# Four gate tiles of a convolution's input as one unit of seven half-size products, behind the query projection

## The chip, the core and the metric

The kernel runs on one core of a Trainium2 chip, as one launch. The metric is the device time of one execution in microseconds (us). A core has five engines that run side by side and wait for each other by semaphores: TensorE (PE in the profile; its weight loads are listed as PEld), VectorE (DVE), ScalarE (ACT), GpSimd (POOL) and SyncE (SP, which here only issues DMAs).

## What is computed

A decoder layer over 512 tokens of width 1024: half a SwiGLU feed-forward step, a token mixer, half a second feed-forward step, and a gated embedding. All inputs and results are float32. The change lies in the mixer:

```python
h = rmsnorm(x, mix_norm[i])
z = h @ w_in[i]
zq, zk, zv, zc, zg = [z[..., offs[j]:offs[j + 1]] for j in range(len(SPLIT_SIZES))]
...
a = sliding_window_attention(q, k, v, sinks[i]) @ attn_proj[i]

ca, cb = jnp.split(zc, 2, axis=-1)
u = ca * jax.nn.sigmoid(cb)
u = causal_depthwise_conv(u, dw_w[i], dw_b[i])
c = jax.nn.silu(layernorm(u, conv_ln_g[i], conv_ln_b[i])) @ conv_proj[i]

ga, gb = jnp.split(zg, 2, axis=-1)
merged = jax.nn.sigmoid(ga) * a + jax.nn.sigmoid(gb) * c
x = x + merged @ w_out[i]
```

There are 16 query heads and 2 key/value heads of 64, a window of 128 tokens, and a depthwise convolution of 31 taps over 1024 channels. `ca` and `cb` are 1024 channels wide each, so 8 tiles of 128 channels.

## The kernel before

**How a product is made.** Activations are kept with channels on the 128 partitions and 512 tokens along the free axis, in 8 tiles (`KD`). Every float32 operand is split into a high part and a rest (`split_into`), and a product is three matmuls: high by high, high by rest, rest by high (`mm3`). A plain projection (`proj`) of one tile of 128 output channels is 8 k-tiles by 3 matmuls of 512 columns into one PSUM bank. Its weight piece is 128 by 1024. For the pieces of `wzc` and `wzg` (`residue`), ACT makes the high part and the negated high part, and a DMA issued by POOL adds the raw piece to the latter; DVE has no part in it.

**A unit.** `unit` computes two by two blocks of weights against two by two blocks of activations with seven products in place of eight, after Strassen's method. Blocks are halves of the contraction and halves of the outputs on the weight side, and halves of the contraction and halves of the tokens (256 each, `lo_` and `hi_`) on the other. The seven sums of the activations are handed to it as `forms`; the seven sums of the weights it makes itself: four blocks are loaded (`raw`, three, and `k`, one), two DMAs add a block onto another, DVE adds into two PSUM tiles (`zs`), and each of the seven is split by ACT (high) and DVE (rest). Products come in the order 1 and 2, 6 and 5, 7 and 3, then 4, each for `nm` = 2 column groups; each is 4 k-tiles by 3 matmuls of 256 columns here. After each pair the caller gets the PSUM banks b1 and b2 and joins them. With nm = 2 a unit holds four such banks beside the two `zs`. Both feed-forward steps, the output projection, half of the query projection (`query_unit`, which also makes the seven sums of the mixer's input) and part of the last gate are made by units.

**The convolution.** Step `a` of channel tile c (`conv_in`) projects ca into a PSUM bank, which stays held (`pas[c]`). Step `b` (`conv_gate`) projects cb, multiplies by the norm's factor `rb2` (DVE), takes the sigmoid (ACT), multiplies by `rb2` again (POOL), multiplies by the held ca into u (DVE), and starts `conv`. `conv` adds the 31 taps: for c = 0, 2, 4 (`POOLCH`) ACT scales (tiles `ct`) and POOL adds; for the other five DVE does each tap in one operation on a PSUM bank (`cz`). Step `L` (`conv_norm`) sums all channels, spreads the mean (`ln_mb` on PE), subtracts it, sums squares (`ln_v_cs`), spreads the reciprocal root (`ln_v_sp`) and makes `cv`, the operand of the last projection of the mixer (`cp`).

**The order.** `ORDER` is a list of steps by hand: K keys and values, Q queries, A scores, E softmax, V values, a and b as above, g and h the two output gates, p the attention's projection, L the layer norm. The steps are only recorded. A planner (`plan`, `simulate`) then lays out all instructions: it has a cost for each kind, a due time for each operation (`deadlines`), a count of buffers (`SLOTS`: 70 general ones of class `a`, 4 `raw`, 4 `hi`, 4 `lo`, 2 `k`, 8 PSUM banks), and for PE it looks up to ten groups of matmuls ahead (`WINDOW`) for one that is ready. It keeps the best of several passes and the instructions are issued in the order that it found. Each engine runs its own in that order, so a late instruction holds up all behind it on its engine. Operations on `nc.flex` go to DVE or POOL as the planner finds best. Where DVE and POOL would both read their shared way to the buffers, it adds a wait of POOL on DVE by hand (`turns`).

Since all instructions are issued at one place, the profile gives L1778 for nearly all of them; they are told apart by the names of their tiles: `ca`, `cb` for the two projections, `wq_a`, `wq_b` for the query unit's two sorts of bank, `q1b` for the other half of the queries, `sc`, `pT`, `o` for attention.

Of the kernel before, what the change touches and what calls it, by code (L numbers as in the profile page):

```python
# [12 lines left out]
AF = mybir.ActivationFunctionType  # L13
ALU = mybir.AluOpType
AX = mybir.AxisListType

P = 128
# [3 lines left out]
KD = D // P  # L21
# [12 lines left out]
PIECE = 1024  # L34
# [3 lines left out]


ORDER = """  # L40
K0 a0 b0 a1 b1 Q0 A0 a3 a2 A1 b2 E0 E1 b3 A2 E2 a4 V0 A3 a5 E3 V1 b4 Q1 V2 b5
V3 A5 a7 A6 g5 h7 A4 E5 A7 E6 E4 V6 g3 a6 E7 g0 V5 b6 V4 g4 g6 V7 h1 g2 h4 b7
g1 p0 p2 g7 p3 L0 p4 h3 p7 h2 p5 p1 p6 h5 h0 h6
"""
POOLCH = (0, 2, 4)
WARM = 9

# [641 lines left out]
def record():  # L689
# [5 lines left out]
    def ftile(name):  # L695
        return nc.tile(name, [P, S], F32, "a")
# [531 lines left out]
    def proj(tag, key, i, h, nk=KD):  # L1228

        w = piece(key, i)  # L1230
        ps = ps_tile(tag)
        with nc.group(tag):
            for k in range(nk):
                mm3(ps, part(w, slice(k * P, (k + 1) * P)), h[k], k == 0, k == nk - 1)
        return ps
# [23 lines left out]
                        mm3(ps, part(w, slice(k * P, (k + 1) * P)), h[k], k == DONE[0], k == DONE[-1])  # L1259
        return {o: ps for o, (w, ps) in out.items()}  # L1260

    us, ys, pas = [None] * KD, [None] * KD, [None] * KD

    def conv_in(c):
        pas[c] = proj(f"ca{c}", "wzc", 2 * c, h2)

    def conv_gate(c):
        pb = proj(f"cb{c}", "wzc", 2 * c + 1, h2)
        sg = ftile(f"sg{c}")
        nc.vector.tensor_tensor(sg, pb, rb2, op=ALU.mult)  # L1270
        nc.scalar.activation(sg, sg, AF.Sigmoid)
        nc.gpsimd.tensor_tensor(sg, sg, rb2, op=ALU.mult)
        us[c] = ftile(f"u{c}")
        nc.vector.tensor_tensor(us[c], pas[c], sg, op=ALU.mult)
        conv(c)

    def conv(c):
        u = us[c]  # L1280
# [35 lines left out]
    def rope(tag, z3, n, tab, t):  # L1316

        w = nc.tile(f"{tag}_w", [P, n, 16], F32, "a")
        cos = tab[:, t, 0].unsqueeze(1).broadcast_to([P, n, 16])
        for d in (0, 8):  # L1320
            sin = tab[:, t, 1, d : d + 8].unsqueeze(1).broadcast_to([P, n, 8])
            nc.gpsimd.tensor_tensor(w[:, :, d : d + 8], z3[:, :, 8 - d : 16 - d], sin, op=ALU.mult)
        nc.gpsimd.tensor_tensor(z3[:, :, 0:16], z3[:, :, 0:16], cos, op=ALU.mult)
        nc.gpsimd.tensor_tensor(z3[:, :, 0:16], z3[:, :, 0:16], w, op=ALU.add)
# [49 lines left out]

    zq, rq = {}, {}

    def query_unit(g):

        forms = {f: [] for f in range(1, 8)}
        for q in range(2):  # L1380
            t5, t6, t7, t4 = (ftile(f"mix_t{n}_{q}") for n in (5, 6, 7, 4))
            for j in range(2):
# [35 lines left out]
    def queries(g):  # L1418

        if g == 0:  # L1420
            query_unit(g)
        else:
            pss = token_major(f"q{g}", "wq", 4 * g, 4, 2, S)
            for t in range(NT):
                z = zq[g, t] = ftile(f"zq{g}_{t}")
                nc.scalar.activation(z, pss[t], AF.Copy, scale=r2k[:, t : t + 1])
        z3s = [zq[g, t].rearrange("p (h d) -> p h d", d=HD) for t in range(NT)]
        rq[g] = heads_rsqrt(f"q{g}", z3s, 8, HD**-0.5, False)
        for t in range(NT):
            rope(f"q{g}_{t}", z3s[t], 8, qcs, t)  # L1430

    state = {}

# [174 lines left out]
    def embedding(i):  # L1608
# [24 lines left out]
        "e": embedding,  # L1633
        "K": lambda n: keys_values(),
        "Q": queries,
        "a": conv_in,
        "b": conv_gate,
        "g": attn_gate,
# [144 lines left out]
def _layout(inputs):  # L1783
# [35 lines left out]
    def pairs(w):  # L1819
        t = kxn(w)  # L1820
        n = t.shape[0] // 2
        return t.reshape(2, n, *t.shape[1:]).transpose(1, 0, 2, 3).reshape(t.shape)

    wap = f["attn_proj"][0].reshape(NH, HD, D)[order].reshape(NH * HD, D)

    half = HD // 8
# [27 lines left out]
        "wd2": wdown(f["ffn2_wdown"][0]),  # L1854
        "wq": wq,
        "wkv": wkv,
        "wzc": pairs(win[:, o[3] : o[4]]),
        "wzg": pairs(win[:, o[4] : o[5]]),
        "gq": rows(f["q_norm"][0]),
        "gk": rows(f["k_norm"][0]),  # L1860
# [35 lines left out]
```

## Time and profile before

| | |
|---|---|
| median of 3 runs | 1145.6 us (1145.52 to 1145.76) |
| the profiled execution | 1145.5 us, of which the profile's span is 1143.8 |
| granted clock of TensorE, mean | 0.999 |
| busy in the span: PE, DVE, ACT, POOL | 99%, 87%, 65%, 40% |
| read from HBM, written | 145.59 MB, 2.10 MB |

Matmuls overlap in time, so the duration of one in the profile (389 ns for 512 columns) is longer than the distance from one to the next. What a group of matmuls costs is read from the chain that ended last, which gives each piece the time until the next one. An engine's idle time costs something only where the chain goes through it.

### The profile page before, as it was taken

The page shows a single profiled execution, that of the slowest core. Times are in us where ns is not written, and L with a number is a line of the kernel's source. Part 1 is how long each engine was busy: PE and PEld are TensorE (multiplying, and loading weights), DVE is VectorE, ACT ScalarE, POOL GpSimd, SP SyncE. Part 2 cuts the span into 40 slices and gives each one's busy share as a digit, 9 for nine tenths or more (in the row PEclk, how much of TensorE's full clock was granted, in tenths as well). Part 3 has the DMA queues.
Part 4 walks back from the last instruction along what each step waited for, and adds up shares of the span by engine and source line. Part 5 has one row for each costly group of instructions (what it writes and reads, how often), then busy time and mean ns, then how long its engine had stood idle before and what let it go on. Part 6 is the DMA issues. An engine that isn't in the chain of part 4 may idle for free.

```text
span 1143.8 us, 20799 instructions
## 1 busy us (share of the span) xinstructions
PE 1135.7 (99%) x7804; PEld 1054.2 (92%) x7804; DVE 1000.4 (87%) x1701; ACT 743.0 (65%) x1332; POOL 457.8 (40%) x531
## 2 busy tenths in 40 slices
PE   9999999999999999999999999999999999999998
PEld 8899999999999988888888888988999999999997
DVE  7799978889887799997997779989998788899897
ACT  7656456665557889999975654655663566565682
POOL 1632113322112896976688124035231132131156
PEclk9999999999999999999999999999999999999999
DMA  7456666665658481664644554436666666656643
GB/s 242 126 162 148 165 160 163 151 144 151 157 132 208 119 206 38 173 158 97 162 129 131 146 148 108 114 108 169 145 164 151 150 167 148 168 119 178 152 117 99
DMA packets 54821, 167.92 MB, mean 147 GB/s; under 512 B 6592, under 2 KB 14400, under 8 KB 54720
## 3 DMA queue, kind: packets, MB, share of 16 engines
q1 hardware_dynamic: 39888, 114.12, 30.2%
q0 software_dynamic: 14688, 52.44, 26.6%
q8 instruction: 61, 1.00, 0.4%
q14 instruction: 40, 0.33, 0.1%
q10 hardware_dynamic: 144, 0.03, 0.0%
HBM read 145.59 MB, written 2.10 MB: 129 GB/s over the span
## 4 chain that ended last, share of the span: by engine, by line
PE 97%; DVE 3%; issue 0%; ACT 0%; ACTq 0%
PE wgu_b L1778 17%; PE wgu_a L1778 13%; PE wd_b L1778 10%; PE wd_a L1778 8%; PE f_g L1778 5%; PE f_u L1778 5%; PE gb L1778 4%; PE ga L1778 4%; PE ap L1778 4%; PE cp L1778 4%; PE ca L1778 3%; PE cb L1778 3%; PE wout_b L1778 2%; PE pg L1778 2%; PE q1b L1778 2%; PE wout_a L1778 2%
## 5 line engine op out<-in xcount | busy, mean ns | idle before, releaser
L1778 DVE TENSOR_TENSOR wlo_wgu<-raw_wgu,whi_wgu 128x1024 fp32r<-128x1024 f32 (+1 forms) x141 | 140.4, 1010 | 27.1 <-ACT whi_wgu L1778 26.8
L1778 ACT ACTIVATE whi_wgu<-raw_wgu 128x1024 fp32r<-128x1024 f32 (+1 forms) x141 | 115.4, 838 | 69.8 <-PE wgu_b L1778 34.7
L1778 POOL TENSOR_TENSOR y<-y,ct 128x511 f32<-128x511 f32 (+26 forms) x90 | 112.0, 1319 | 14.1 <-ACT ct L1778 5.3
L1778 PE MATMUL wgu_b<-f_t_h,wlo_wgu 128*128 128x256 f32 x408 | 115.5, 283 | 0.0
L1778 PE MATMUL wgu_b<-f_t_h,whi_wgu 128*128 128x256 f32 x408 | 115.5, 283 | 0.0
L1778 PE MATMUL wgu_b<-f_t_l,whi_wgu 128*128 128x256 f32 x408 | 115.5, 283 | 0.0
L1778 ACT ACTIVATE whi_wd<-raw_wd 128x896 fp32r<-128x896 f32 (+1 forms) x60 | 59.3, 989 | 73.3 <-PE wd_b L1778 41.5
L1778 DVE SCALAR_TENSOR_TENSOR cz<-u,dww,cz 128x504 f32<-128x504 f32 (+28 forms) x145 | 104.7, 733 | 2.0
L1778 POOL DMA_DIRECT2D raw_wgu<-in_wgu x34 | 29.7, 878 | 153.3 <-DMA raw_wgu<-in_wgu 78.6
L1778 PEld LDWEIGHTS wgu_b<-f_t_h,wlo_wgu 128*128 128x128 f32 x408 | 78.3, 192 | 0.0
L1778 PEld LDWEIGHTS wgu_b<-f_t_h,whi_wgu 128*128 128x128 f32 x408 | 78.3, 192 | 0.0
L1778 PEld LDWEIGHTS wgu_b<-f_t_l,whi_wgu 128*128 128x128 f32 x408 | 78.3, 192 | 0.0
L1778 DVE TENSOR_TENSOR wlo_wd<-raw_wd,whi_wd 128x896 fp32r<-128x896 f32 (+1 forms) x60 | 70.8, 1180 | 7.2 <-ACT whi_wd L1778 6.8
L1778 PE MATMUL wgu_a<-f_nh,wlo_wgu 128*128 128x256 f32 x272 | 77.0, 283 | 0.0
L1778 PE MATMUL wgu_a<-f_nh,whi_wgu 128*128 128x256 f32 x272 | 77.0, 283 | 0.0
L1778 PE MATMUL wgu_a<-f_nl,whi_wgu 128*128 128x256 f32 x272 | 77.0, 283 | 0.0
L1778 PE MATMUL wd_b<-f_f_h,wlo_wd 128*128 128x256 f32 x264 | 75.1, 285 | 1.2 <-DVE x L1778 1.2
L1778 PE MATMUL wd_a<-f_f_h,wlo_wd 128*128 128x256 f32 x264 | 74.7, 283 | 0.0
L1778 PE MATMUL wd_a<-f_f_h,whi_wd 128*128 128x256 f32 x264 | 74.7, 283 | 0.0
L1778 PE MATMUL wd_b<-f_f_l,whi_wd 128*128 128x256 f32 x264 | 74.7, 283 | 0.0
L1778 PE MATMUL wd_b<-f_f_h,whi_wd 128*128 128x256 f32 x264 | 74.7, 283 | 0.0
L1778 PE MATMUL wd_a<-f_f_l,whi_wd 128*128 128x256 f32 x264 | 74.7, 283 | 0.0
(625 smaller groups left out, 4278.6 us busy)
## 6 DMA issues: line engine op xcount, KB each, us to landing
raw_wgu<-in_wgu SPq DMA_DIRECT2D x76, 512.0 KB, 4.5
raw_wgu<-in_wgu POOLq DMA_DIRECT2D x34, 512.0 KB, 5.5
raw_wd<-in_wd SPq DMA_DIRECT2D x32, 448.0 KB, 4.0
raw_wd<-in_wd SPq DMA_DIRECT2D x16, 512.0 KB, 4.4
raw_wzc<-in_wzc SPq DMA_DIRECT2D x16, 512.0 KB, 3.9
wlo_wzc<-raw_wzc POOLq DMA_DIRECT2D x16, 512.0 KB, 4.9
raw_wzg<-in_wzg SPq DMA_DIRECT2D x16, 512.0 KB, 3.5
wlo_wzg<-raw_wzg POOLq DMA_DIRECT2D x16, 512.0 KB, 4.5
```

Source lines behind the costliest of these rows:

```text
L1778: made[op] = getattr(engines[op.eng], op.what)(*a, **k)
```

## The change

The gates (cb) of channel tiles 2, 3, 4 and 5 leave their four steps `b2` to `b5` and become one step `U0`, a unit that stands right behind the first half of the queries, `Q0`. It takes the same seven sums of the mixer's input (`forms2`, made by `query_unit`). The four weight pieces are laid out anew on the host, so that each holds half of the contraction for two tiles. The unit leaves sigmoid gates in SBUF (`su2` to `su5`); the four steps `a2` to `a5` then multiply and convolve as soon as their own projection is there. The other gates (0, 1, 6, 7) stay as they are.

```diff
 ORDER = """
-K0 a0 b0 a1 b1 Q0 A0 a3 a2 A1 b2 E0 E1 b3 A2 E2 a4 V0 A3 a5 E3 V1 b4 Q1 V2 b5
+K0 a0 b0 a1 b1 Q0 U0 A0 a3 a2 A1 E0 E1 A2 E2 a4 V0 A3 a5 E3 V1 Q1 V2
 V3 A5 a7 A6 g5 h7 A4 E5 A7 E6 E4 V6 g3 a6 E7 g0 V5 b6 V4 g4 g6 V7 h1 g2 h4 b7
 g1 p0 p2 g7 p3 L0 p4 h3 p7 h2 p5 p1 p6 h5 h0 h6
 """
+UNITED = (2, 3, 4, 5)
...
     def conv_in(c):
         pas[c] = proj(f"ca{c}", "wzc", 2 * c, h2)
+        if c in UNITED:
+            convolve(c)
 
     def conv_gate(c):
         pb = proj(f"cb{c}", "wzc", 2 * c + 1, h2)
-        sg = ftile(f"sg{c}")
+        sg = sgs[c] = ftile(f"sg{c}")
         nc.vector.tensor_tensor(sg, pb, rb2, op=ALU.mult)
         nc.scalar.activation(sg, sg, AF.Sigmoid)
         nc.gpsimd.tensor_tensor(sg, sg, rb2, op=ALU.mult)
+        convolve(c)
+
+    def convolve(c):
         us[c] = ftile(f"u{c}")
-        nc.vector.tensor_tensor(us[c], pas[c], sg, op=ALU.mult)
+        nc.vector.tensor_tensor(us[c], pas[c], sgs[c], op=ALU.mult)
         conv(c)
...
+    forms2 = {f: [] for f in range(1, 8)}
+
     def query_unit(g):
 
-        forms = {f: [] for f in range(1, 8)}
+        forms = forms2
...
+    def gate_unit():
+
+        def src(b):
+            return Dram("wzc")[2 * UNITED[2 * (b // 10 - 1) + b % 10 - 1] + 1]
+
+        def finish(sg):
+            nc.flex.tensor_tensor(sg, sg, rb2, op=ALU.mult)
+            nc.scalar.activation(sg, sg, AF.Sigmoid)
+            nc.gpsimd.tensor_tensor(sg, sg, rb2, op=ALU.mult)
+
+        for f, m, b1, b2 in unit("gu", src, PIECE, lambda k, m: (m * 4 + k) * P, forms2):
+            if f == 1:
+                t, u = (ftile(f"su{UNITED[n]}") for n in (m, m + 2))
+                sgs[UNITED[m]], sgs[UNITED[m + 2]] = t, u
+                nc.scalar.copy(t[:, lo_], b1)
+                nc.vector.tensor_tensor(t[:, lo_], b2, t[:, lo_], op=ALU.add)
+            t, u = sgs[UNITED[m]], sgs[UNITED[m + 2]]
+            if f == 6:
+                nc.scalar.copy(t[:, hi_], b2)
+                nc.scalar.activation(u[:, hi_], b1, AF.Copy, scale=-1.0)
+            elif f == 7:
+                nc.vector.tensor_tensor(t[:, hi_], b1, t[:, hi_], op=ALU.add)
+                nc.vector.scalar_tensor_tensor(u[:, hi_], b2, -1.0, u[:, hi_], op0=ALU.mult, op1=ALU.add)
+                finish(t)
+            elif f == 4:
+                nc.scalar.activation(u[:, lo_], b2, AF.Copy, scale=-1.0)
+                finish(u)
...
+        "U": lambda n: gate_unit(),
...
+    at = [2 * u + 1 for u in UNITED]
+    wzc = pairs(win[:, o[3] : o[4]])
+    wu = wzc[at].reshape(2, 2, P, 2, 4, P).transpose(0, 3, 2, 1, 4, 5)
+    wzc[at] = wu.reshape(4, P, PIECE)
```

More of the change, by code (lines that the diff above doesn't have):

```diff
@@ L1260, in proj2 @@
         return {o: ps for o, (w, ps) in out.items()}
-    us, ys, pas = [None] * KD, [None] * KD, [None] * KD
+    us, ys, pas, sgs = ([None] * KD for _ in range(4))
     def conv_in(c):
         pas[c] = proj(f"ca{c}", "wzc", 2 * c, h2)
+        if c in UNITED:
+            convolve(c)
     def conv_gate(c):
         pb = proj(f"cb{c}", "wzc", 2 * c + 1, h2)
-        sg = ftile(f"sg{c}")
+        sg = sgs[c] = ftile(f"sg{c}")
         nc.vector.tensor_tensor(sg, pb, rb2, op=ALU.mult)
@@ L1856, in _layout @@
         "wkv": wkv,
-        "wzc": pairs(win[:, o[3] : o[4]]),
+        "wzc": wzc,
         "wzg": pairs(win[:, o[4] : o[5]]),
```

## The prediction

> **What bounds the kernel now.** I read the page's first part and its chain of work first, then what TensorE (PE) waited for over the whole span, then windows over the mixer.
>
> ```profile
> PE 1135.7 (99%) x7804; PEld 1054.2 (92%) x7804; DVE 1000.4 (87%) x1701; ACT 743.0 (65%) x1332; POOL 457.8 (40%) x531
> PE 97%; DVE 3%; issue 0%; ACT 0%; ACTq 0%
> PE wd_b L1778 <- DVE x L1778: 1.2, 4, 0.5
> PE ca L1778 <- DVE s L1778: 0.9, 1, 0.9
> 345.88:704.62 358.74, 357.60 (x1893) 301.60 (x1892) 310.15 (x562) 285.62 (x564) 235.71 (x304) 1.00 0.55 140
> ```
>
> PE is busy 99% of the span and is 97% of the chain that ended last. The last line is the mixer, from the first key/value matmul to the last of the convolution's projection; its columns are length, then busy time of PE, PEld, DVE, ACT and POOL, granted clock, DMA share and GB/s. PE idles 358.74 - 357.60 = 1.14 us there, at a granted clock of 1.00. So time is won in this stage only by giving PE less to stream, or from those 1.14 us, of which 0.9 us is one projection waiting for a PSUM bank that VectorE (DVE) had to empty of scores. DVE is second with 310 of 359 us.
>
> **What the change takes from PE.** The chain of waits, in order of time, has both forms of work: a query unit of seven products (wq) that is already in the kernel, and gate projections (cb).
>
> ```profile
> 381.00 1.43 PE wq_b L1778 x12
> ...
> 396.82 1.44 PE wq_a L1778 x12
> 398.26 5.47 PE ca L1778 x24
> 403.73 2.87 PE wq_b L1778 x24
> 406.60 5.47 PE cb L1778 x24
> ...
> 443.88 5.46 PE cb L1778 x24
> ...
> 450.67 5.46 PE cb L1778 x24
> ```
>
> One gate tile is 8 x 3 = 24 matmuls of 512 columns and costs 5.46 us, 0.2275 each. Four of them (the fourth lies at a place where the chain runs over DVE; I give it the same) cost 2 x 5.46 + 5.47 + 5.46 = 21.85 us. The new unit has the query unit's count: 7 products x 2 column groups x 4 k-tiles x 3 = 168 matmuls of 256 columns. The query unit ran six products from 381.00 to 398.26, without a gap, and the seventh in 2.87: 17.26 + 2.87 = 20.13 us, 0.1198 each. **PE saves 21.85 - 20.13 = 1.72 us**, all of it on the path that ends last.
>
> Why an eighth less arithmetic gives no eighth (2.73 us): from 0.2275 = a + 512 b and 0.1198 = a + 256 b, a column costs b = 0.42 ns and a matmul a = 12 ns whatever its width. The change removes 96 x 512 - 168 x 256 = 6144 columns (2.6 us) and adds 72 matmuls (0.9 us).
>
> The Trainium skill, page "TensorE: Matmul & The Clock Gate", section "Back-to-back issue gap", has a fixed part of 2.5 ns and N / 2.4 ns of streaming; by it the saving would be, as an estimate, 96 x 215.8 - 168 x 109.2 ns = 2.4 us. This trace shows 227.5 and 119.8 ns in place of these, so by the trace the narrow form pays more, and that speaks against the change.
>
> **What it adds beside PE.** The same unit's rows, grouped by form, in the stretch that prepares the query unit (362 to 398), and the rows of the gates:
>
> ```profile
> L1778 DVE TENSOR_TENSOR wlo_wq<-raw_wq,whi_wq 128x1024 fp32r<-128x1024 f32 x5 | 7.3, 1478 | 0.8 <-ACT whi_wq L1778 0.7
> L1778 DVE TENSOR_TENSOR wlo_wq<-zs_wq,whi_wq 128x512 fp32r<-128x512 f32 x4 | 2.7, 685 | 0.6 <-ACT whi_wq L1778 0.6
> L1778 DVE TENSOR_TENSOR zs_wq<-raw_wq,raw_wq 128x512 f32<-128x512 f32 x2 | 1.4, 695 | 0.0
> L1778 DVE TENSOR_TENSOR zs_wq<-raw_wq,zs_wq 128x512 f32<-128x512 f32 x2 | 1.4, 688 | 0.0
> L1778 DVE SCALAR_TENSOR_TENSOR zq<-wq_b,mix_n_r,zq x2: 472/474/475, 385.6 to 389.4; 128x256 f32<-128x256 f32 x2
> L1778 DVE TENSOR_TENSOR sg<-cb,mix_n_rb x8: 677/683/691, 370.5 to 577.1; 128x512 f32<-128x512 f32 x8
> L1778 ACT ACTIVATE whi_wq<-raw_wq 128x1024 fp32r<-128x1024 f32 x5 | 5.4, 1077 | 0.8 <-ACT zq L1778 0.5 <-ACT ct L1778 0.3
> L1778 ACT ACTIVATE whi_wq<-zs_wq 128x512 fp32r<-128x512 f32 x4 | 2.3, 598 | 1.9 <-PE cb L1778 1.9
> L1778 ACT ACTIVATE whi_wzc<-raw_wzc x16: 1042/1049/1061, 343.4 to 509.3; 128x1024 fp32r<-128x1024 f32 x16
> L1778 ACT ACTIVATE zq<-wq_a,mix_minus 128x256 f32<-128x256 f32 x2 | 0.9, 462 | 0.4 <-PE wq_a L1778 0.4
> ```
>
> DVE: preparing seven weight forms costs 7.3 + 2.7 + 1.4 + 1.4 = 12.8 us, where the four gate pieces had none on DVE (their rest is made by ACT and an adding DMA). Joining the products adds 6 half-width operations of 0.47 (2.8 us). The multiplication by the norm stays, 4 x 0.68 us, if the planner leaves it on DVE (it is now free to go to POOL). So DVE gets 12.8 + 2.8 = 15.6 us more, or 12.9 if POOL takes it. ACT: weights 5.4 + 2.3 in place of 8 x 1.05 = 8.4, and 8 half-width copies of 0.46: 3.0 us more. POOL loses two of four DMA issues. The input's seven forms cost nothing, since the query unit makes them; they live some 20 us longer in 16 of the 70 "a" buffers. DMA moves 6 pieces of 512 KB where it moved 8. The conversions of u are the same ones, earlier.
>
> What hides them, by windows that cover the place of the change and what follows (columns as above):
>
> ```profile
> 381.00:401.00 20.00, 20.00 (x157) 19.51 (x157) 16.81 (x26) 18.70 (x30) 18.21 (x18) 1.00 0.58 139
> 401.00:421.00 20.00, 19.86 (x121) 16.89 (x120) 19.69 (x42) 17.04 (x26) 19.38 (x28) 1.00 0.90 212
> 421.00:460.00 39.00, 38.00 (x229) 31.05 (x229) 38.44 (x74) 36.94 (x101) 27.74 (x44) 1.00 0.29 76
> 460.00:520.00 60.00, 60.00 (x329) 49.67 (x327) 55.59 (x115) 59.43 (x131) 47.66 (x66) 1.00 0.66 162
> 520.00:582.00 62.00, 62.00 (x307) 51.49 (x307) 53.26 (x92) 59.19 (x131) 45.41 (x65) 1.00 0.50 125
> ```
>
> The new unit will run at about 401 to 421. DVE is full there (19.69 of 20, then 38.44 of 39). What gives way is the depthwise convolution, whose taps (cz) fill DVE wherever nothing is due; it is wanted only by the layer norm near 625 (rows below). From 381 to 460 DVE has 3.19 + 0.31 + 0.56 = 4.1 us free, so some 11.5 us of taps move behind 460; from 460 to 582 it has 4.41 + 8.74 = 13.2 us free. The taps can use it, because all four gates are now known at about 425 rather than at 457. ACT's 3 us fall on 381 to 421, with 1.30 + 2.96 us free.
>
> If that cover fails, the layer norm is late. Its slack, from DVE's and PE's rows in order of time:
>
> ```profile
> 625.00 0.69 DVE L1778 TENSOR_TENSOR ln_s_l<-ln_acc,ln_s_h 128x512 fp32r<-128x512 f32 x1 [3.74 <-ACT ln_s_h L1778]
> 638.13 2.29 DVE L1778 TENSOR_TENSOR ln_v_sq<-ln_v_sq,ln_v_sq 128x512 f32<-128x512 f32 x2
> 647.90 0.69 DVE L1778 TENSOR_TENSOR ln_v_dgl<-ident,ln_v_cs 128x512 fp32r<-128x512 f32 x1
> 662.67 1.30 DVE L1778 TENSOR_TENSOR cv_l<-y,cv_h 128x512 fp32r<-128x512 f32 x2 [0.24 <-ACT cv_h L1778]
> 631.10 0.46 PE ln_mb L1778 x2
> 642.48 1.68 PE ln_v_cs L1778 x16
> 649.77 0.45 PE ln_v_sp L1778 x2
> 661.10 43.52 PE cp L1778 x192
> ```
>
> Its operands are ready at 625.7, 640.4, 648.6 and 664.0; PE takes them at 631.10, 642.48, 649.77 and (eighth k-tile of the first cp tile, 21 matmuls in) 661.10 + 4.8 = 665.9. Those waits are 5.4 + 2.1 + 1.2 + 1.9 = 10.6 us that the convolution may be late without PE seeing it, 8.9 once PE itself is 1.7 earlier.
>
> **The sum.** The profiled execution took 1145.5 us, 1.7 more than its span, and the median is 1145.6. Work: -1.72. Waits: the 0.9 us bank wait may go, since the input halves (ca2 to ca5) no longer hold a bank until their gate is done. The new unit itself can wait, because DVE prepares its weights while full and its six banks leave little room for the first scores. That wait is not in the trace: below, it is -1.14 us (all of the mixer's idle time gone), since PE can't idle less than never; above, the unit could wait for a whole form's preparation at each of its seven forms, 12.8 us. Nearest is the query unit, with DVE beside it nearly as full: no gap. I take the waits as unchanged, 0, and get 1145.6 - 1.7 = **1143.9 us**.
>
> **Rivals.**
> 1. *The waits go too.* With the banks free the 0.9 us vanishes, perhaps all 1.14. For it: the waiting projection stood behind scores in a stage with three or four projections parked in banks. Against: DVE, which empties those banks, gets more. 1143.9 - 0.9 to 1.14 = 1142.8 to 1143.0.
> 2. *The unit waits for DVE.* One or two forms come late by one full-width subtraction queued behind another (1.5 each) or the first scores do. For it: 98% busy DVE at 401 to 460. Against: the query unit had no gap, and taps can be put back. Price 1.5 to 3: 1145.4 to 1146.9, no change.
> 3. *DVE becomes the bound (slower).* The place is the wait of ln_mb and then cp for the convolution's end. The 15.6 us are added, and taps find none of the free time because it lies in waits that a fixed order can't use. It decides from 8.9 us of delay on: with 15.6, PE stands 6.7 us, and 1143.9 + 6.7 = 1150.6; with a quarter of the free 13.2 us used, 1147.3. Against: the free time lies where taps are queued. A port rule makes it likelier: of eight full-width query subtractions the shortest took 1.215, the median 1.474 and the longest 2.310 us, with POOL working beside them, so a bad placement adds up to 5 x (2.31 - 1.48) = 4.2 us.
> 4. *It doesn't do what it says*: PE streams the new unit as slowly per column as some wider form, so that nothing is saved. The query unit's rows leave no room for that; no chance is set aside.
>
> ```profile
> L1778 DVE TENSOR_TENSOR wlo_wq<-raw_wq,whi_wq x8: 1215/1474/2310, 366.5 to 471.6; 128x1024 fp32r<-128x1024 f32 x8
> ```
>
> The Trainium skill, page "SBUF — State Buffer", section "Who interferes with whom", says that a VectorE operation with two SBUF inputs and a GpSimd operation that reads SBUF exclude each other for a whole instruction. By that rule each of the five subtractions could cost a POOL addition's length more; the spread from 1.215 to 2.310 us agrees with it.
>
> **Chances.** Forecast 0.42 (of it 0.07 under 1143.3), rival 1 0.28, rival 2 0.16 (of it 0.03 over 1147.9), rival 3 0.14, with a fifth of it under 1147.9. What this kernel's measurement can tell from no change is 0.2%, 2.3 us: faster is under 1143.3, slower over 1147.9. Faster 0.07 + 0.28 = 0.35; slower 0.03 + 0.11 = 0.14, raised to 0.17 because the fixed orders of all engines are planned anew and a few us can be lost where I see none; same 0.48. The range goes from 1142.4 (rival 1, with 0.4 us of slow starts gone too) to 1147.9, leaving out most of rival 3.
>
> **What would show it.** Right: wq and the new unit's products in groups of 1.44 us one after the other, 20.1 us in sum; PE idle in the mixer near 1.1 us; mixer length near 357.0; DVE busy there near 323 to 326 us. Wrong: PE waiting for the unit's low parts near 400 to 420, or for qT or scores (rival 2); PE waiting for ln_mb, ln_v_cs or cp with DVE full until then (rival 3); or differences outside the mixer, where the sum has none.

## The result: slower by 6.5 us

| | median, us | runs |
|---|---|---|
| before | 1145.67 | 1145.52 to 1145.76, 4 runs |
| after | 1152.18 | 1151.77 to 1152.36, 4 runs |

The ratio of after to before is 1.0056, with a 95% interval of 1.0039 to 1.0074. The forecast was 1143.9, with a range up to 1147.9: the result lies outside it, on the other side.

### The profile after

The first part of the page and its chain of work, of the changed kernel:

```profile
PE 1137.9 (99%) x7876; PEld 1057.8 (92%) x7876; DVE 1009.7 (88%) x1719; ACT 743.5 (65%) x1341; POOL 463.9 (40%) x530
PE 94%; DVE 2%; ACT 2%; issue 1%; DMA 0%; ACTq 0%
```

PE still looks full. The share that tells is that of the chain: ACT had 0% of it and now has 2%, and PE went from 97% to 94%. What PE waited for between 300 and 760 us, in the changed kernel, the three largest (us in total, times, longest):

```profile
PE pT L1813 <- POOL s L1813: 2.5, 1, 2.5
PE o L1813 <- DVE s L1813: 0.8, 1, 0.8
PE wout_a L1813 <- DVE mg_l L1813: 0.7, 1, 0.7
```

The largest wait is new: transposes of the softmax's result (pT) wait 2.5 us for the POOL operation that scales it. The windows of the changed kernel (columns as in the prediction) show where it lies, and what follows it:

```profile
346.03:710.30 364.27, 359.70 (x1964) 305.41 (x1964) 319.60 (x580) 286.12 (x573) 242.54 (x304) 1.00 0.52 135
...
450.00:460.00 10.00, 7.05 (x58) 5.02 (x55) 9.55 (x20) 9.67 (x32) 7.78 (x13) 0.94 0.16 54
460.00:465.00 5.00, 5.00 (x19) 3.98 (x19) 4.47 (x9) 5.00 (x12) 4.79 (x4) 0.78 0.28 89
```

The mixer is 364.27 us long, 5.5 more than before. PE idles 4.57 us in it (1.14 before), 2.95 of them in 450 to 460. In the five microseconds behind that the mean granted clock is 0.78. That is the mean of a stretch at half clock and one at full clock, which the last section shows. The second half of the queries (q1b) runs just there. The chain, first after, then before, has it (start, us):

```profile
459.51 23.10 PE q1b L1813 x96
666.78 43.52 PE cp L1813 x192
```

```profile
460.67 21.79 PE q1b L1778 x96
```

PE begins q1b 1.2 us *earlier* than before, takes 1.3 us longer for it, and is 5.7 us late at the first matmul of cp (661.10 before).

**Where the 6.6 us of the two profiled spans (1143.8 and 1150.4) went.** I added up, over all PE rows of the timeline from the first kvb matmul to the first of cp, the time from each row's start to the next row's start, by tile. Idle time that the view gives with a releaser is kept apart.

| PE's time, us | before | after | difference |
|---|---|---|---|
| gate projections: cb, and the unit's gu_a and gu_b | 44.00 | 21.77 + 20.50 | **-1.73** |
| waits with a releaser | 0.88 | 4.19 | +3.31 |
| transposes of the softmax (pT, 64) | 6.25 | 8.14 | +1.89 |
| second half of the queries (q1b, 96) | 21.86 | 23.29 | +1.43 |
| values (o, 56) | 13.16 | 13.68 | +0.52 |
| all else | 229.07 | 229.18 | +0.11 |
| sum | 315.22 | 320.75 | +5.53 |

Another 0.15 us were lost ahead of this stretch, and from there to the end of the span another 0.9, at the start of the output projection. The unit saved what it was meant to save, and 7.2 us of waits, of slow transposes and values and of a lower clock came with it. Of the +3.3 us of waits, 1.8 stand ahead of q1b; the other 1.5 are four waits at 495 to 557 us, in the second group of heads, where the kernel before has none.

The unit itself in the chain of the changed kernel:

```profile
401.29 1.44 PE gu_b L1813 x12
...
408.52 1.67 PE gu_a L1813 x12
...
415.95 2.88 PE gu_b L1813 x24
...
424.74 2.87 PE gu_b L1813 x24
```

Products of 1.44 us (one of 1.67) stand one after another from 401.29 to 418.83, and the last takes 2.87: 20.4 us.

Then the chain at the first softmax. Of the changed kernel:

```profile
443.32 5.49 PE ca L1813 x24
448.81 0.44 PE pT L1813 x4
449.24 1.67 PE sc L1813 x24
450.92 0.64 ACT s L1813 x2
...
452.10 3.81 ACT s L1813 x16
...
458.24 0.56 PE pT L1813 x3
```

Of the kernel before, over the same stretch (cb at 443.88 and 450.67 has been shown):

```profile
428.83 5.74 PE ca L1778 x24
434.57 1.62 PE sc L1778 x24
...
437.51 5.47 PE ca L1778 x24
...
449.80 0.87 PE pT L1778 x8
```

Before, projections stand between scores (sc) and transposes (pT), and the chain never leaves PE after 428.8. After, the last projection (ca) ends at 448.8, and from 450.9 to 458.2 the chain runs over ACT: copies of scores and values, the exponentials, and its own scaling of two of the eight heads. The listed wait of 2.5 us is for the other six, which POOL scales. The softmax itself is no slower. POOL's rows with the name s, of six 128 by 128 scalings each, for the first two tiles, before and then after:

```profile
434.96 2.11 POOL L1778 TENSOR_SCALAR s<-s,den 128x128 f32<-128x128 f32 x6 [0.59 <-DVE den L1778]
443.58 2.10 POOL L1778 TENSOR_SCALAR s<-s,den 128x128 f32<-128x128 f32 x6
```

```profile
442.29 2.12 POOL L1813 TENSOR_SCALAR s<-s,den 128x128 f32<-128x128 f32 x6 [0.34 <-DVE den L1813]
456.64 2.12 POOL L1813 TENSOR_SCALAR s<-s,den 128x128 f32<-128x128 f32 x6 [0.35 <-DVE den L1813]
```

The first tile of scores starts at 418.33 before and at 427.54 after, by PE's timeline, and its scaling starts 16.6 and 14.8 us later; the second starts at 425.67 and 441.04, and its scaling starts 17.9 and 15.6 us later. So a softmax tile takes some 15 to 18 us in either kernel. What differs is what PE has to do meanwhile: between the first scores and q1b it runs five plain projections before (cb, ca, ca, cb, cb) and three after (ca, ca, ca).

### The profile page after: what moved, and what is told of

Same layout as the page of the kernel before. It is cut to its first block, busy times and chain, and to the rows that moved or that the text cites. A ratio compares the mean times of both kernels' runs of the same rounds, so it can differ in the third digit from the quotient of the medians.

```text
span 1150.4 us, 20984 instructions
## 1 busy us (share of the span) xinstructions
PE 1137.9 (99%) x7876; PEld 1057.8 (92%) x7876; DVE 1009.7 (88%) x1719; ACT 743.5 (65%) x1341; POOL 463.9 (40%) x530
## 4 chain that ended last, share of the span: by engine, by line
PE 94%; DVE 2%; ACT 2%; issue 1%; DMA 0%; ACTq 0%
PE wgu_b L1813 17%; PE wgu_a L1813 13%; PE wd_b L1813 10%; PE wd_a L1813 8%; PE f_g L1813 5%; PE f_u L1813 5%; PE ca L1813 4%; PE ap L1813 4%; PE cp L1813 4%; PE gb L1813 3%; PE ga L1813 3%; PE q1b L1813 2%; PE pg L1813 2%; PE wout_b L1813 2%; PE cb L1813 2%; PE wout_a L1813 1%
## 5 line engine op out<-in xcount | busy, mean ns | idle before, releaser
L1813 POOL TENSOR_TENSOR y<-y,ct 128x511 f32<-128x511 f32 (+28 forms) x90 | 111.0, 1294 | 22.7 <-DVE cz L1813 4.3
L1813 DVE SCALAR_TENSOR_TENSOR cz<-u,dww,cz 128x507 f32<-128x507 f32 (+22 forms) x145 | 100.5, 730 | 0.7
```

Of the source, the lines that this page charges most:

```text
L1813: made[op] = getattr(engines[op.eng], op.what)(*a, **k)
```

## The experiments

The theory at the start was **cover**: the four gates were the PE work under which the first softmax was hidden, and the unit does that work ahead of the first scores. Its rivals: the unit's load on DVE, the unit's banks, and the order of all engines that is planned anew with any change. Times of the kernel before beside these runs were 1145.6 to 1145.8.

### 1. The gates moved without a unit (e1)

The changed kernel with gates 2 to 5 as four plain projections at the unit's place:

```diff
+GATES = (2, 3, 4, 5)
...
+    def gates():
+        for c in GATES:
+            gate_only(c)
+
     def conv_gate(c):
+        gate_only(c)
+        convolve(c)
+
+    def gate_only(c):
         pb = proj(f"cb{c}", "wzc", 2 * c + 1, h2)
...
-        convolve(c)
...
-        "U": lambda n: gate_unit(),
+        "U": lambda n: gates(),
...
-    wu = wzc[at].reshape(2, 2, P, 2, 4, P).transpose(0, 3, 2, 1, 4, 5)
-    wzc[at] = wu.reshape(4, P, PIECE)
```

> The changed kernel, but the gates 2 to 5 are four plain projections again, made one after the other at the place of the unit (layout of their weights as before). So only the move is left: no seven products, no weight sums on VectorE, no four banks held by a unit. Cover theory (TensorE has nothing ready during the first softmaxes, because 21.8 us of projections that used to stand there now run ahead of the first scores): the wait before the second tile's transposes near 457 stays, 2 us or more, the granted clock falls behind it, and the time is that of the changed kernel plus the 1.7 us that the unit saves, 1152 to 1154 us. VectorE theory (the 15.6 us that the unit adds to VectorE delay scores and softmax) and bank theory (the unit's banks hold the first scores off): no such wait, 1145 to 1147 us.

Measured: 1152.43 (1152.31 to 1152.66), ratio 1.0058 [1.0041, 1.0075]. The largest wait of PE, and the window behind it, of this kernel:

```profile
PE pT L1821 <- POOL s L1821: 3.0, 1, 3.0
```

```profile
460.00:465.00 5.00, 4.83 (x15) 3.52 (x16) 4.94 (x12) 5.00 (x14) 4.29 (x8) 0.50 0.02 3
```

The same wait at the same place, a fall of the clock, the same time, with no unit, none of its weight preparation on DVE and none of its banks. **The move makes the loss, not the unit.** Unit against four plain gates at one place is 0.25 us in the medians. At the first matmul of cp the unit is 1.5 us ahead (666.6 against 668.1 by the timelines), and 0.9 of that it gives back at the output projection, where this kernel loses nothing.

### 2. DVE relieved (e2)

The changed kernel without 28 of the 31 taps of channels 1 and 3 (its output lacks them):

```diff
-        for d in [*range(2, TAPS), 1] if ext else range(1, TAPS):
+        for d in ([2, 1] if c in (1, 3) else [*range(2, TAPS), 1]) if ext else range(1, TAPS):
```

> The changed kernel without 28 of the 30 later taps of the convolution's channel tiles 1 and 3, which run on VectorE from 390 on: some 2 x 28 x 0.66 = 37 us less on VectorE, more than twice what the unit added. Its output lacks these taps. VectorE theory: the waits of TensorE between 450 and 460 go, and the time falls to 1145 us or less. Cover theory: the softmax is a chain on ScalarE and the supply of projections is as small as before, so TensorE still idles 2 us or more between 440 and 460; what is gained is gained elsewhere, and the time stays above 1148 us.

Measured: 1149.33 (1148.9 to 1150.38), ratio 1.0034 [1.0022, 1.0046]. PE still has 3.7 us of waits between the first scores and q1b, spread over qTp, o and pT, and the clock of 460 to 465 is still 0.80; what was gained, 2.9 us, lies later. So the wait at the first softmax is not DVE's load. DVE's load is worth something elsewhere, though more was taken off it here (its busy time in the span went from 1009.7 to 982.2 us, 27.5 less, where 37 had been expected) than the unit put on it.

### 3. and 4. The idle time filled with matmuls that nobody reads (e3, e6)

The changed kernel with 11, then 8 matmuls into the bank of the second tile's transposes, ahead of them:

```diff
+            if (g, t, hh) == (0, 1, 0):
+                with nc.group("idle"):
+                    for _ in range(11):
+                        nc.tensor.matmul(pt, ones_r, seen[-1][1], start=True, stop=True)
```

> The changed kernel with 11 matmuls of 512 columns (2.5 us) that nobody reads, put into the bank of the second tile's transposes before these, and made to wait for the first tile's split probabilities, so that they fall into the wait near 455. If the wait costs twice, by its length and by the lower clock that is granted after it (0.78 from 460 to 465, and 23.1 in place of 21.8 us for the second half of the queries), the clock stays at 1.00 there, that half takes 21.8 us, and the time falls by 1 to 2 us to 1150 to 1151 us although work was added. If the clock fell for another reason, it falls again and the time stays at 1152 us or rises.

> As the filled wait before, with 8 matmuls (1.8 us) in place of 11, since the 11 shifted the softmax behind them and the wait opened again at 460. If a wait here costs a second time by the lower clock granted after it, and this one is short enough, the clock stays at 1.00 from 460 to 465 and the second half of the queries takes 21.8 us in place of 23.1. If the clock falls whatever the length of the wait, that half again takes 22.5 us or more.

Measured: 1154.11 with 11 (ratio 1.0073 [1.0053, 1.0093]) and 1154.09 with 8 (1.0072). Neither took the idle time away: the waits opened again behind the added matmuls (up to q1b, pT waits 1.9 us in two pieces in the run with 11, and 1.6 in the run with 8), and the clock in 460 to 465 was 0.77 and 0.76. So the time rose as the second branch of the first expectation says, and the clock fell, but waits were there again: whether the clock would have stayed up without them can't be read from these two runs. They are inconclusive.

### 5. Half of the gates moved: gates 2 and 3 (e4)

As in the first experiment, with two gates, and b4 and b5 in their old places in the order:

```diff
-UNITED = (2, 3, 4, 5)
+UNITED = (2, 3)
+GATES = (2, 3)
...
-K0 a0 b0 a1 b1 Q0 U0 A0 a3 a2 A1 E0 E1 A2 E2 a4 V0 A3 a5 E3 V1 Q1 V2
+K0 a0 b0 a1 b1 Q0 U0 A0 a3 a2 A1 E0 E1 A2 E2 a4 V0 A3 a5 E3 V1 b4 Q1 V2 b5
```

> As the run with plain gates at the unit's place, but only the gates 2 and 3 stand there; b4 and b5 stay where the kernel before has them, as two plain projections between the values and the second half of the queries. TensorE's work is that of the kernel before. Cover theory: what counts is what is left to run while the first softmaxes run, and the kernel before already had b2 and b3 ahead of that stretch (406 to 426) and b4 and b5 in it (444 to 456); so nothing or little is lost, 1145.5 to 1147.5 us, with the granted clock at 1.00 from 460 to 465. If instead each moved gate costs its share (6.6 us / 4), the time is 1149 us.

Measured: 1153.33 (1151.49 to 1153.52), ratio 1.0062 [1.0049, 1.0076]. Cover had foretold far less, and it fails here: PE has five projections between the first scores and q1b, as before. The waits of this kernel, and the chain that leads to q1b:

```profile
PE qTp L1821 <- DVE s L1821: 1.9, 1, 1.9
PE o L1821 <- POOL po_1l L1821: 1.3, 1, 1.3
PE o L1821 <- POOL po_1h L1821: 1.1, 1, 1.1
```

```profile
456.83 2.39 POOL wlo_wq L1821
459.22 0.34 POOL po_1h L1821
...
459.97 1.28 POOL sg L1821
461.25 0.60 POOL po_1l L1821
```

The masked probabilities (po_1h, po_1l), 0.3 and 0.6 us of the chain, stand in POOL's fixed order behind a weight subtraction of 2.39 us and a gate's multiplication of 1.28, and q1b stands in PE's fixed order behind the values (o) that need them. Another engine's order makes the wait, with cover in plenty.

### 6. The unit in another order (e5)

The changed kernel with another order of steps:

```diff
-K0 a0 b0 a1 b1 Q0 U0 A0 a3 a2 A1 E0 E1 A2 E2 a4 V0 A3 a5 E3 V1 Q1 V2
-V3 A5 a7 A6 g5 h7 A4 E5 A7 E6 E4 V6 g3 a6 E7 g0 V5 b6 V4 g4 g6 V7 h1 g2 h4 b7
+K0 a1 a0 b0 b1 Q0 U0 A0 A1 a2 E0 E1 a3 A2 a4 V0 E2 A3 V1 a5 Q1 V2 E3
+V3 A5 a7 A6 h7 g5 A4 A7 E5 a6 E7 E6 V7 g3 g0 b6 V5 V6 E4 V4 g6 g4 h1 g2 h4 b7
```

> The changed kernel with another list of steps, and nothing else: the second tile's scores and the first softmaxes stand ahead of a2 and a3, a4 and a5 stand later, and the second group's softmaxes and values are arranged anew, so that projections are left for the first softmaxes. Cover theory: the unit's own saving of 1.7 us against plain gates comes out, TensorE's idle time in the mixer falls from 4.6 to 2 us or less and the time is 1143.5 to 1146 us. If the unit itself (its load on VectorE or its banks) is what costs, a new order changes little: 1150 us or more.

Measured: 1148.29 (1148.02 to 1148.93, 11 runs), ratio 1.0023 [1.0014, 1.0032]. The window behind the place of the wait:

```profile
460.00:465.00 5.00, 5.00 (x24) 4.14 (x23) 4.76 (x10) 5.00 (x23) 4.65 (x6) 1.00 0.34 108
```

Four projections lie between the first scores and q1b, the waits there are 0.6 us in all, and the clock stays at 1.00. 3.9 of the 6.5 us are back with the unit unchanged, so the unit alone does not make the loss. But the time lies between the two ranges that were expected, and the unit is still not ahead; at 538 us a value product waits 1.4 us.

### 7. to 9. The kernel before, with one exchange each (e7, e8, e10)

Gate 5 and the values of the third tile (e7), the projection a2 and the second tile's scores (e8), gate 3 and the third tile's scores (e10); the old line first, then the three new ones in this order:

```diff
-K0 a0 b0 a1 b1 Q0 A0 a3 a2 A1 b2 E0 E1 b3 A2 E2 a4 V0 A3 a5 E3 V1 b4 Q1 V2 b5
+K0 a0 b0 a1 b1 Q0 A0 a3 a2 A1 b2 E0 E1 b3 A2 E2 a4 V0 A3 a5 E3 V1 b4 Q1 b5 V2
+K0 a0 b0 a1 b1 Q0 A0 a3 A1 a2 b2 E0 E1 b3 A2 E2 a4 V0 A3 a5 E3 V1 b4 Q1 V2 b5
+K0 a0 b0 a1 b1 Q0 A0 a3 a2 A1 b2 E0 E1 A2 b3 E2 a4 V0 A3 a5 E3 V1 b4 Q1 V2 b5
```

> The kernel before with two neighbouring steps of its list exchanged (b5 ahead of V2), with no unit and nothing moved ahead of the scores: how much the list alone does. Cover theory: the supply during the first softmaxes is the same, so the time stays within 2 us of 1145.6. If any touch of the list costs as much as the change did, the loss was not the move's: 1150 us or more.

> The kernel before, with one exchange in its hand-written order: the second tile's scores (A1) stand ahead of the projection a2. All gates stay in their old steps, no unit, so PE has the same work and as much of it around the first softmax as before. Theory 1 (the loss of the change is a lack of ready PE work, since the four gates no longer stand between the first scores and the first values): the supply is unchanged, so no loss, 1145.3 to 1147. Rival (the loss comes from how all engines' fixed orders fall out around the first scores, values and the second half of the queries, whatever the supply): PE waits for transposes or values near 450 to 465 by 3 us or more, the granted clock in the next 5 us falls under 0.9, the second half of the queries (q1b) takes over 22.3 us, and the time is 1149 to 1153.

> The kernel before with gate 3 (b3) behind the third tile's scores (A2) instead of ahead of them. Same work, no unit. Theory 1 (supply): a projection stands one step later, nearer to the wait for the first values, so no loss and perhaps the one wait of 0.9 us for a bank goes: 1144.8 to 1145.8. Rival (any exchange around the first scores lays all engines' orders anew, at a cost): 1147 or more, with PE waiting in 420 to 465 by over 2 us. Either way it says how much of the change's loss an order alone can make or save.

Measured: the first 1145.86 (ratio 1.0001 [0.9992, 1.0009]), the second **1156.44** (1.0093 [1.0079, 1.0107]), the third 1147.02 (1.0011 [1.0002, 1.0020]). In the first, PE runs the same sequence from the first scores to q1b. The third fits neither expectation: the time is at the rival's lower end, but PE waits 1.1 us in 420 to 465, not over 2, and for a bank, as before. In the second, all the kernel's work is what it was, no gate is moved by hand, and the loss is 10.8 us, more than the change's. Its largest wait, and two windows:

```profile
PE pT L1778 <- POOL s L1778: 3.1, 1, 3.1
```

```profile
440.00:460.00 20.00, 16.90 (x109) 13.46 (x108) 18.41 (x40) 18.05 (x52) 9.63 (x21) 0.91 0.00 0
460.00:465.00 5.00, 5.00 (x17) 3.40 (x16) 4.60 (x9) 4.45 (x8) 4.83 (x6) 0.67 0.33 108
```

The cover theory had expected no loss, since the list keeps the supply. But the list is not the order: the planner started the first scores at 429.68, 11 us later than before, with projections ahead of them, and only three were left between them and q1b. It is the same wait as in the changed kernel, though not all of the loss: cp takes 47.2 us there in place of 43.5. So what counts is what the planner leaves behind the first scores, not what the list names there.

### 10. Half of the gates moved: gates 4 and 5 (e9)

> The changed kernel with only gates 4 and 5 at the unit's place, as two plain projections; gates 2 and 3 stay in their old steps behind the first scores. Theory 1 (supply): two of the four projections are missing between the first scores and the second half of the queries, but the two that remain are the ones that stand nearest to the first softmax, so half of the loss or less, 1146.5 to 1149.5. Rival (order of all engines around 440 to 465, whatever the supply, as the run with gates 2 and 3 moved suggests): a wait of PE for transposes or values of 2 us or more there, a granted clock under 0.9 in 460 to 465, and 1151 to 1154.

Measured: 1150.09 (1150.01 to 1151.27), ratio 1.0040 [1.0026, 1.0053]. Five projections lie behind the first scores, no wait at all in 440 to 465, clock 1.00: the rival's wait did not come. The time is 0.6 us beyond what cover allowed, because PE waits later on:

```profile
482.00:520.00 38.00, 36.59 (x198) 29.64 (x198) 34.76 (x71) 37.80 (x68) 34.35 (x43) 1.00 0.58 139
520.00:563.00 43.00, 41.04 (x229) 33.80 (x226) 40.60 (x79) 40.36 (x100) 28.12 (x43) 1.00 0.56 135
```

3.4 us of PE are idle there, in the second group of heads.

### 11. and 12. The unit, with one more projection ahead of q1b (e11, e12)

The changed kernel with g0 in front of Q1 (e11), and the order of e5 with g5 in front of A3 (e12); each is taken out of its later place:

```diff
-K0 a0 b0 a1 b1 Q0 U0 A0 a3 a2 A1 E0 E1 A2 E2 a4 V0 A3 a5 E3 V1 Q1 V2
+K0 a0 b0 a1 b1 Q0 U0 A0 a3 a2 A1 E0 E1 A2 E2 a4 V0 A3 a5 E3 V1 g0 Q1 V2
```

```diff
-K0 a1 a0 b0 b1 Q0 U0 A0 A1 a2 E0 E1 a3 A2 a4 V0 E2 A3 V1 a5 Q1 V2 E3
+K0 a1 a0 b0 b1 Q0 U0 A0 A1 a2 E0 E1 a3 A2 a4 V0 E2 g5 A3 V1 a5 Q1 V2 E3
```

> The changed kernel with one step moved in its hand-written order: g0 (one projection of the output gate, 5.5 us of PE work that waits for nothing in attention) stands ahead of the second half of the queries (Q1) instead of 21 steps later. Theory 1 as narrowed by the runs so far (what counts is how many projections PE still has between the first scores, sc, and the second half of the queries, q1b: three in the changed kernel, with the gates moved without a unit, and in the kernel before with its scores exchanged, each with a wait of 2.5 to 3.1 us for the transposes; five in the kernel before, without one): with four, the wait of pT for POOL goes under 1 us, the granted clock in the 5 us ahead of and behind q1b's start stays over 0.95, q1b takes 21.8 to 22.1 us, and the time is 1147.5 to 1150. Rival (any new order pays as much, whatever stands between): waits of 2 us or more in 445 to 466, the clock falls, and 1151 to 1154.

> The changed kernel in the new order that gave 1148.3 us (four projections between the first scores and q1b), with g5 moved ahead of A3 so that there are five, as in the kernel before. Theory 1 as narrowed: no wait over 0.5 us in 440 to 465, clock 1.00, q1b 21.8 us. The unit's 1.7 us are then won in that stretch, and the first matmul of cp starts at or ahead of 661.1 (kernel before), if the waits do not come back at 480 to 600; time 1144.5 to 1147. Rival (the waits only move to the second group of heads, since POOL, ACT and DVE have the same work and PE has one projection less there): waits of 2 us or more in 480 to 600, and 1147.5 to 1150.

Measured: 1150.90 (ratio 1.0045 [1.0030, 1.0060]) and 1152.29 (1.0057 [1.0041, 1.0074]). At the place both came out as cover says: with four projections 1.2 us of small waits and a clock of 1.00, with five no wait and a clock of 1.00. In time both missed, the second by 5 us. The window of the second at the place is full:

```profile
440.00:460.00 20.00, 20.00 (x132) 16.65 (x130) 19.94 (x32) 19.53 (x55) 16.16 (x22) 1.00 0.27 86
460.00:465.00 5.00, 5.00 (x25) 4.05 (x22) 4.94 (x11) 4.80 (x13) 4.72 (x5) 1.00 0.37 118
```

Its largest loss is at the layer norm, 3.6 of the 6.4 us between the two spans; 1.9 were lost ahead of cp, where the attention's projection waits 2.0 us at 586, and 0.9 behind it, at the output projection. The chain of the second kernel there, over ACT in steps of 0.71 + 0.52 us per channel tile:

```profile
662.61 0.71 ACT y L1811
663.32 0.52 ACT cv_h L1811
...
670.82 4.18 PE cp L1811 x17
```

and the operations on the convolution's sum, first of this kernel, then of the one before (ns; first and last start):

```profile
L1811 DVE TENSOR_TENSOR ln_acc<-ln_acc,y x1: 1064/1064/1064, 617.7 to 617.7; 128x512 f32<-128x512 f32 x1
...
L1811 POOL TENSOR_TENSOR ln_acc<-ln_acc,ln_acc x1: 1298/1298/1298, 633.4 to 633.4; 128x512 f32<-128x512 f32 x1
```

```profile
L1778 DVE TENSOR_TENSOR ln_acc<-ln_acc,y x1: 693/693/693, 618.8 to 618.8; 128x512 f32<-128x512 f32 x1
...
L1778 POOL TENSOR_TENSOR ln_acc<-ln_acc,ln_acc x1: 1287/1287/1287, 623.0 to 623.0; 128x512 f32<-128x512 f32 x1
```

DVE's channels are done at 618.8 and 619.5, alike in both. POOL's last addition is 10.4 us later, and the projection behind it, cp, is fed tile by tile: it takes 47.1 us up to the next product where it took 43.5. In the changed kernel POOL's last addition is 6.2 us later than before (629.2), and cp takes its 43.52 us: PE itself comes 5.7 us late there.

### 13. and 14. What sets the layer norm back (e13, e14)

The last order without the taps of channels 1 and 3 (as in e2), and the last order with four plain gates (as in e1):

> The changed kernel in the last run's order (five projections between the first scores and q1b), without 28 of the 31 taps of convolution channels 1 and 3, so that its output lacks them and VectorE (DVE) has some 37 us less. In the last run no wait was left at 440 to 465, but the convolution's projection (cp) took 47.1 us from its first matmul to the next product's, 3.6 over the kernel before, and the layer norm's sum stood 10.6 us later (ln_s_l at 635.65 against 625.00). If VectorE's load by the unit is behind that (rival 3 of the prediction): cp takes 43.5 to 44.0 and the time is 1146 to 1148. If it is GpSimd (POOL), whose last channel's taps ended at 631 in that trace while VectorE's had ended at 618.5: cp still takes 45.5 us or more, ln_s_l stays behind 632, and the time is 1149.5 to 1152.5.

> The last run's order, but gates 2 to 5 as four plain projections at the unit's place: neither the unit's weight preparation nor its joins are on VectorE, PE has 1.7 us more. If the unit itself sets the layer norm back: cp takes 43.5 to 44.0 us. If the order does it: cp takes 45 us or more, or a wait comes back somewhere else, and the time stays within 2.5 us of the last run's 1152.3.

Measured: 1151.98 (ratio 1.0054 [1.0037, 1.0071]) and 1155.77 (1.0089 [1.0074, 1.0104]). In both, cp takes 43.52 us, and yet neither gains more than 0.3 us on the last order: the losses stand elsewhere. So neither expectation fits as a whole: in the first kernel cp is fast as for DVE's load, but the time is that of the POOL branch; the second lies 3.5 us from the last run's time, where 2.5 had been allowed. The first kernel's sum of the convolution is as late as ever, which speaks against DVE's load:

```profile
L1811 DVE TENSOR_TENSOR ln_s_l<-ln_acc,ln_s_h x1: 693/693/693, 635.9 to 635.9; 128x512 fp32r<-128x512 f32 x1
```

but PE is late itself (first matmul of cp at 667.1), with 2.4 us idle and a clock of 0.92 in 520 to 563, so cp does not see it. The second has 3.1 us of idle PE in 482 to 563 and another 2.0 in 563 to 600. Each edit let the planner lay everything out anew, and the loss turned up at another place.

### All runs side by side

Plain projections that start between the first scores and q1b; waits with a releaser in that stretch; mean granted clock in 460 to 465; median. From PE's timeline and the windows of each kernel. In the kernel before, e7 and e10 nearly all of the waits are one for a bank (ca behind DVE s), not for the softmax.

| kernel | projections | waits, us | clock | time, us |
|---|---|---|---|---|
| changed kernel | 3 | 2.7 | 0.78 | 1152.2 |
| e1, gates moved, no unit | 3 | 4.0 | 0.50 | 1152.4 |
| e2, less DVE | 3 | 3.7 | 0.80 | 1149.3 |
| e3, e6, filled | 3 | 3.0, 2.0 | 0.77, 0.76 | 1154.1 |
| e8, before, scores exchanged | 3 | 3.1 | 0.67 | 1156.4 |
| e5, unit, other order | 4 | 0.6 | 1.00 | 1148.3 |
| e11, unit, g0 forward | 4 | 1.2 | 1.00 | 1150.9 |
| e14, e12 without unit | 4 | 0 | 1.00 | 1155.8 |
| before | 5 | 0.9 | 1.00 | 1145.6 |
| e7, before, b5 and V2 | 5 | 1.0 | 1.00 | 1145.9 |
| e10, before, b3 and A2 | 5 | 1.1 | 1.00 | 1147.0 |
| e9, gates 4 and 5 moved | 5 | 0 | 1.00 | 1150.1 |
| e12, unit, g5 forward | 5 | 0 | 1.00 | 1152.3 |
| e13, e12 with less DVE | 5 | 0 | 1.00 | 1152.0 |
| e4, gates 2 and 3 moved | 5 | 3.2 | 0.71 | 1153.3 |

The first three columns go together: with three projections there is the wait and the fall of the clock, in every one of six kernels, with or without a unit (e3 and e6 are the changed kernel with matmuls added); with four or five the clock stays up there and no wait is over 1.1 us, but for e4, whose wait comes from POOL's order. The clock also falls at other places: at 513 us in e4, 541 in e6, 556 in e13 and 567 in e14. The last column does not follow the first. With the wait cured, other places take their share: every kernel whose order at the first scores was laid out anew lost 1.4 to 10.8 us somewhere, and the kernel before, with 0.9 us of waits from the keys to cp, is the exception.

## Why the prediction was wrong

**The term that failed** is the one of the waits: "I take the waits as unchanged, 0". It measured +3.3 us of listed waits up to cp, +1.9 and +0.5 of transposes and values that were stretched, +1.4 of lower clock in q1b, and +0.9 at the output projection. The reasoning behind it looked for the wait in the wrong place. It asked whether the new unit would wait, found the query unit beside a full DVE without a gap, and was right: no product of the unit was more than 0.23 us late (1.67 for 1.44). But a step that is moved also leaves a hole. The prediction's own chain showed cb at 443.88 and 450.67, behind the first scores; both left, and what would then stand late behind the first softmax was not worked out. From rows of before it could have been: a softmax tile takes 17 to 18 us from its scores to its scaling, five projections of 5.5 us stood in that stretch, and three of them are gates that the diff takes out (the fourth ran ahead of the scores).

**The saving on PE was right.** Foretold 1.72 us, measured 1.73. That it agrees to a hundredth is luck: the unit took 20.4 us in the chain and 20.5 from start to start (20.13 foretold), and the four gates 22.2 (21.85 foretold), both some 0.4 more. The cost of 12 ns per matmul, which makes an eighth less arithmetic worth 8% of the time, fits this result.

**DVE** got 9.4 us more in the mixer (310.15 to 319.60), not 12.9 to 15.6. That is less than foretold, in part because of the 13 subtractions for the query weights POOL did three in place of one (all nine of the unit's were on DVE). It did not decide: with 27.5 us taken off DVE, the waits stayed.

**Rival 1** (the waits go too): the 0.9 us wait for a bank did go, and larger ones came.

**Rival 2** named "the first scores" as what might come late, which they did, by 9.2 us. Its price of 1.5 to 3 us was that of one or two late subtractions and its cause DVE; what followed was a hole in PE's work, and the whole loss is more than twice the price.

**Rival 3** was on the right side and at the wrong place in the changed kernel, where nothing waits for ln_mb or cp. Its mechanism exists: in e12, once the first wait is cured, cp is fed late and takes 3.6 us more. But the engine that comes last there is POOL, whose last addition starts 14.6 us behind DVE's end (3.5 in the kernel before), and the prediction's slack of 8.9 us was reckoned with DVE's load alone.

**The chance of a loss by a new layout** was put at 0.03 ("the fixed orders of all engines are planned anew"). The runs e7, e8 and e10 price that: one exchange in a list, with no other change, cost 0.2, 10.8 and 1.4 us. One of three lost more than the change did; on three runs, 0.03 was too little.

**What stays open.** That the move alone makes the loss is shown (e1), and that the wait at the first softmax goes with the number of projections left behind the first scores is shown in both directions (e8; e5, e11, e12). How much of the 6.5 us the first softmax alone makes is not shown: with that wait cured, 3.9 us came back in e5, 1.3 in e11 and none in e12. Why each new order loses time at some later place, in the second group of heads, at the layer norm or at the output projection, is read from the traces and was not settled: each edit that was to isolate it changed the whole order. No order was found in which the unit beats the kernel before; that there is none isn't shown. Instructions kept in the order of before, with the unit alone put in by hand, were not tried.

## What to carry to other kernels

A matmul stream that is 99% busy hides its latencies under particular pieces of work: before moving one, find the long chain on other engines that runs beneath it, and count what is left over it. A saving of 1.7 us on the full engine is worth making only together with the order around it, since in this kernel, with PE 99% busy, one exchange of two steps cost as much as 10.8 us. And a list of steps is not the order that runs: read the order from the trace, and test an exchange alone before reading a change's effect through it.

## What the runs showed of the hardware

**The clock falls to half after short waits, for 3.4 us at a time.** Windows of the changed kernel whose bounds lie where the clock changes:

```profile
458.77:462.18 3.41, 3.39 (x10) 2.79 (x10) 3.04 (x7) 3.41 (x6) 2.12 (x1) 0.50 0.00 0
462.18:470.00 7.82, 7.82 (x36) 6.42 (x36) 6.71 (x13) 7.82 (x27) 7.45 (x10) 1.00 0.52 160
```

The clock is 0.50 for 3.41 us, and 1.00 behind that; 0.78 is only the mean of a window that holds 2.2 us of it. The stretch is as long in e2, e3, e4 and e6, and twice as long, 6.83 us, in e1 and e8, so the clocks in the table above say how much of it falls into 460 to 465, not how deep the fall is. In it the matmuls of q1b start 0.42 us apart in place of 0.23. q1b runs 3.0 us of the stretch; at half speed that is, as an estimate from these numbers, 1.5 us lost, and 1.4 were measured. The waits that led to it were short: the longest was 2.5 us in the changed kernel, 3.0 in e1, 3.1 in e8, 1.6 in e6, 1.3 in e2 and e4 and 1.2 in e3, each amid transposes, scores and value products. Waits of 0.6 us (e5) and 1.2 us in three pieces (e11) left the clock at 1.00. The Trainium skill, page "TensorE: Matmul & The Clock Gate", section "What's actually happening", lets the clock halve after an idle window of about 3.4 us. The half agrees with the trace, and the stretch at half clock is one or two such windows long; but no single wait here was as long as that.

**A stream can starve without a listed wait.** In e12 cp took 3.6 us longer, while the window over it shows PE full and the list of waits has nothing for cp:

```profile
655.00:715.00 60.00, 59.93 (x270) 46.97 (x269) 51.18 (x71) 34.53 (x50) 16.76 (x14) 1.00 0.40 106
```

Two of its rows in the timeline (start, us):

```profile
668.30 0.50 PE L1811 MATMUL cp<-cv_l,whi_wcp 128*128 128x512 f32 x1
668.80 0.50 PE L1811 MATMUL cp<-cv_h,wlo_wcp 128*128 128x512 f32 x1
```

Matmuls overlap: a row lasts 0.39 us, and the next one starts 0.23 us after it when nothing is missing. Here the three matmuls of one channel tile take 1.23 us up to the next three in place of 0.68; the missing time shows as rows of 0.50 us that start up to 0.50 apart, and not as idle time. Starts, not busy time, tell what a stream lost.

**Two SBUF operands, with POOL at work, cost DVE more than one from PSUM.** The gate's multiplication by the norm's factor reads its tile from SBUF now, where it read PSUM at 0.683 us:

```profile
L1813 DVE TENSOR_TENSOR su<-su,mix_n_rb x4: 683/1206/1624, 415.7 to 429.3; 128x512 f32<-128x512 f32 x4
```

Three of the four ran beside a POOL addition of a tap and took 1.16 to 1.62 us; the one without took 0.683. The eight in the kernel before, which read PSUM, took 0.677 to 0.691, though POOL was at work beside seven of them. That is 2.0 us more in all, which the prediction had put at nothing.
